# V of all four head pairs in one product of 512 columns: a change to a hybrid attention and state-space layer

## The chip, the core and the metric

The kernel runs on one core of a Trainium2 chip. The core has a matrix engine (TensorE, PE in the rows; its loads of stationary operands are PEld), a vector engine (VectorE, DVE), an activation engine (ScalarE, ACT), a general engine (GpSimd, POOL) and a queue engine (SyncE, SP) that only issues DMAs. Each engine runs its own list of instructions in order and waits on semaphores. The metric is device time in microseconds of one execution.

## The reference, cut to what matters

A decoder layer over 2048 tokens of width 1024. One projection gives Q, K and V for 3 attention groups of 8 heads of width 64 (windows 128, 512, 2048 with dilations 1, 4, 16), a gate `z_a`, the state-space input `u_s`, its gate `z_s`, and two merge gates:

```python
proj = einsum('bld,de->ble', h, w_in)
q, k, v = proj[..., :1536], proj[..., 1536:3072], proj[..., 3072:4608]   # (3 groups, 8 heads, 64) each
attn = _dilated_mixture(q, k, v) * silu(z_a)       # each group a causal dilated band, mixed by softmax sums
y = gelu(_s5(u_s, ...)); y = y * sigmoid(y @ w_glu + b_glu) * silu(z_s)
out = (sigmoid(g_a) * (attn @ w_attn_up) + sigmoid(g_s) * (y @ w_ssm_up)) @ w_o
h = layer_norm(2**0.25 * h + out) * ln_g + ln_b
```

The change touches how V, of shape (tokens, 3 x 512), is computed, and when `u_s` and the two branch gates are.

## The kernel before, in words

Arithmetic is float32 by splitting: an operand is cast to a short form `hi`, the rest `lo = raw - hi` is kept beside it, and each product is three matmuls, hi x hi, hi x lo and lo x hi. The tokens are worked in two halves `h` of 1024. Both forms of the half's x lie in SBUF (`X["h", kt]`, `X["l", kt]`, eight tiles of 128 model channels).

**Weights** come as blocks of 128 x 1024 numbers (512 KB) from one list, `plan` (L724 to 740), strictly in its order. The class `Weights` (L124 to 203) loads a block into a ring of two raw tiles (`fetch`, the DMA is issued on ACT's queue, L137), casts it to `hi` in two halves of 512 columns on ACT (`part`, L172), and subtracts to `lo` on POOL (L175; in the last phase on DVE). `hi` and `lo` have rings of two as well. A consumer calls `take` for a block, and while it runs `ahead` (first half of the next block's split) and `ahead2` (second half, then the DMA of the block after that).

**A projection block** (`gemm`, L205 to 248) makes 128 output channels for the 1024 tokens: two halves of 512 tokens, 8 model tiles, 3 matmuls of 512 columns each, 48 in all, into one of two PSUM banks `proj` per half. A piece of work of 6 such matmuls is one unit, 1.296 us in the kernel's own account. Q, K, `u`, `z_a`, `z_s` and gates are such blocks.

**V** (`v_gemm`, L431 to 458) is transposed: x is stationary, the weight moves, tokens are the output rows. One call makes V of two head pairs (256 columns) for the half's eight token tiles, from two weight blocks: block one holds model tiles 0 to 3, block two 4 to 7. Four token tiles share two banks, so that block one feeds 48 matmuls of 256 columns before block two is wanted. It is called for pairs 0 and 2 of each group, 12 times; results go through tile `th` to DRAM (`vD`), and each pair's job loads its 128 columns from there (`load_v`), into its tile `VV`.

**The jobs.** For each half, pair (0 to 3) and group (0 to 2), `job_proj` (L363) makes V if the pair is even, Q, then K (into tile `KC`); ACT casts and DVE subtracts out of PSUM (L398, L400). `job_attn` does the attention of a job in ten steps: scores (L595, L597), row maximum on DVE (L602), exp on ACT (L606), transposes on PE (L614), copies on ACT and DVE (L616, L617), PV (L625). The generator `interleave` (L261) deals out a job's projections (`bulk`) and the attention of the job before (`side`, 16.0 units) so that both end together: this fixes the order on every engine's list, and the side goes first where they tie. The main loop (L959 to 983) puts one `z` block into each job of the odd pairs. So a job of an even pair has V, Q and K, and one of an odd pair Q, K and a `z` block.

**The start.** `first_blocks` makes two `u` blocks while x is loaded and split; then come two more `u` blocks and the job (0, 0) without attention. Beside them DVE builds the tables of the state-space branch (`s5_tables`), a chain of some 200 small instructions, dealt out by `interleave` from the 17th unit on.

## Time and profile before

| | |
|---|---|
| time, median of 3 runs | 2165.84 us (2164.9 to 2165.98) |
| the profiled execution's own time | 2166.9 us |
| its span, first to last instruction | 2165.1 us |
| PE busy | 2136.9 us, 99% of the span |
| DVE, ACT, POOL busy | 1191.5, 1007.5, 701.4 us |
| mean granted TensorE clock | 0.998 |
| V products (L446), 2304 matmuls of 256 columns | busy 221.0 + 218.3 + 217.2 us |

The rows give start, duration, engine and line of an instruction, what it writes and reads, and in square brackets the idle time before it and what ended that. Matmuls overlap, so a matmul's duration (0.28 or 0.39 us) says little; what one costs is the distance from its start to the next one's. "ACTq" and "SPq" are DMA issues.

### The profile page before, as it was taken

The page shows a single profiled execution, that of the slowest core. Times are in us where ns is not written, and L with a number is a line of the kernel's source. Part 1 is how long each engine was busy: PE and PEld are TensorE (multiplying, and loading weights), DVE is VectorE, ACT ScalarE, POOL GpSimd, SP SyncE. Part 2 cuts the span into 40 slices and gives each one's busy share as a digit, 9 for nine tenths or more (in the row PEclk, how much of TensorE's full clock was granted, in tenths as well). Part 3 has the DMA queues.
Part 4 walks back from the last instruction along what each step waited for, and adds up shares of the span by engine and source line. Part 5 has one row for each costly group of instructions (what it writes and reads, how often), then busy time and mean ns, then how long its engine had stood idle before and what let it go on. Part 6 is the DMA issues. An engine that isn't in the chain of part 4 may idle for free. (4 is left out here: it accounts for less than half of the span.)

```text
span 2165.1 us, 32183 instructions
## 1 busy us (share of the span) xinstructions
PE 2136.9 (99%) x11440; PEld 1822.2 (84%) x11440; DVE 1191.5 (55%) x3064; ACT 1007.5 (47%) x2355; POOL 701.4 (32%) x587
## 2 busy tenths in 40 slices
PE   8999999999999999999999999999999999999998
PEld 6998889998888999888998888888888878888786
DVE  6644554445553244555445555258887784358725
ACT  3255665556554355665555665233433362232222
POOL 2322253253342234243243352411100004322643
PEclk9999999999999999999999999999999999999999
DMA  6323344344374333434344334554345463533721
GB/s 177 112 92 99 109 127 127 95 127 118 104 218 111 94 101 122 124 101 110 98 140 112 110 108 119 171 169 137 113 147 162 123 216 127 161 112 117 262 88 78
DMA packets 227569, 278.12 MB, mean 128 GB/s; under 512 B 89553, under 2 KB 175441, under 8 KB 227409
## 3 DMA queue, kind: packets, MB, share of 16 engines
q10 hardware_dynamic: 91776, 143.81, 21.7%
q1 hardware_dynamic: 135632, 132.25, 20.7%
q8 instruction: 91, 1.49, 0.3%
q14 instruction: 70, 0.57, 0.1%
HBM read 189.24 MB, written 74.19 MB: 122 GB/s over the span
## 5 line engine op out<-in xcount | busy, mean ns | idle before, releaser
L215 PE MATMUL proj<-xh,whi 128*128 128x512 f32 x1600 | 645.5, 403 | 1.2 <-ACT gt L719 1.2
L215 PE MATMUL proj<-xh,wlo 128*128 128x512 f32 x1600 | 628.5, 393 | 0.0
L215 PE MATMUL proj<-xl,whi 128*128 128x512 f32 x1600 | 626.0, 391 | 0.0
L175 POOL TENSOR_TENSOR wlo<-wraw,whi 128x512 fp32r<-128x512 f32 (+1 forms) x266 | 353.5, 1340 | 533.4 <-ACT whi L172 505.6
L215 PEld LDWEIGHTS proj<-xh,wlo 128*128 128x128 f32 x1600 | 300.2, 188 | 65.5
L215 PEld LDWEIGHTS proj<-xh,whi 128*128 128x128 f32 x1600 | 301.6, 189 | 54.4 <-issue 1.5
L215 PEld LDWEIGHTS proj<-xl,whi 128*128 128x128 f32 x1600 | 301.3, 188 | 51.3
L606 ACT ACTIVATE Sx<-Sx,st 128x256 f32<-128x256 f32 (+1 forms) x384 | 181.3, 473 | 263.7 <-DVE st L602 253.3
L633 POOL TENSOR_TENSOR og<-ot 128x128 f32<-128x128 f32 x192 | 88.2, 459 | 534.5 <-DVE ot L632 522.5
L172 ACT CAST whi<-wraw 128x512 fp32r<-128x512 f32 (+1 forms) x328 | 194.8, 617 | 117.4 <-PE ob L1406 43.3
L617 DVE TENSOR_TENSOR PT<-tr,PT 128x512 fp32r<-128x512 f32 (+1 forms) x192 | 118.9, 619 | 221.2 <-ACT PT L616 221.0
L446 PE MATMUL proj<-whi,xh 128*128 128x256 f32 x768 | 221.0, 288 | 0.0
L446 PE MATMUL proj<-wlo,xh 128*128 128x256 f32 x768 | 218.3, 284 | 0.9 <-POOL wlo L175 0.8
L446 PE MATMUL proj<-whi,xl 128*128 128x256 f32 x768 | 217.2, 283 | 0.0
L446 PEld LDWEIGHTS proj<-wlo,xh 128*128 128x128 f32 x768 | 146.8, 191 | 2.9 <-POOL wlo L175 2.4
L446 PEld LDWEIGHTS proj<-whi,xh 128*128 128x128 f32 x768 | 146.7, 191 | 0.1
L446 PEld LDWEIGHTS proj<-whi,xl 128*128 128x128 f32 x768 | 146.7, 191 | 0.0
L602 DVE CUSTOM_DVE_ANT_0 Sx<-sca,bias 128x256 f32<-128x256 f32 (+1 forms) x192 | 74.6, 388 | 105.3 <-PE sca L597 101.9
L632 DVE TENSOR_TENSOR ot<-ob,ot 64x256 f32<-64x256 f32 x192 | 81.0, 422 | 83.5 <-ACT ot L630 72.8
L632 DVE TENSOR_TENSOR ot<-oa,ot 64x256 f32<-64x256 f32 x192 | 81.0, 422 | 74.5 <-ACT ot L630 63.0
L614 PE MATMUL tr<-ident,Sx 128*128 128x128 f32 x664 | 109.9, 276 | 5.6 <-ACT Sx L606 5.1
L400 DVE TENSOR_TENSOR KC<-proj,KC 64x512 fp32r<-64x512 f32 x96 | 66.1, 688 | 82.9 <-ACT KC L398 82.0
(319 smaller groups left out, 3779.0 us busy)
## 6 DMA issues: line engine op xcount, KB each, us to landing
wraw<-in_w_in_dram ACTq DMA_DIRECT2D x102, 512.0 KB
ld<-gD SPq DMA_DIRECT2D x32, 512.0 KB
gD<-gt ACTq DMA_DIRECT2D x27, 512.0 KB
wraw<-in_w_v_dram ACTq DMA_DIRECT2D x24, 512.0 KB
vD<-th ACTq DMA_DIRECT2D x48, 256.0 KB
cB<-coefD SPq DMA_DIRECT2D x48, 256.0 KB
VV<-vD SPq DMA_DIRECT2D x16, 512.0 KB
xr<-in_xT_dram SPq DMA_DIRECT2D x16, 512.0 KB
```

Of the source, the lines that this page charges most:

```text
L172: A.copy(hi[:, c], raw[:, c])
L175: eng.tensor_tensor(lo[:, c], raw[:, c], hi[:, c].bitcast(F32), op=OP.subtract)
L215: T.matmul(ps, w[:, wc], m(kt)[:, cols], start=kt == 0 and n == 0, stop=3 * kt + n == last)
L400: V.tensor_tensor(gdst(lo, g, t), gsrc(ps[rows[s]], g), gdst(hi[rows[s]].bitcast(F32), g, t), op=OP.subtract)
L446: T.matmul(o, X[m, kt][:, 128 * i:128 * i + 128], w[half_k][wx][:, wc], start=kt == 0 and n == 0 and t % 2 == 0, stop=kt == 7 and n == 2, ...
L602: V.tensor_tensor_reduce(sx[:, s, lo:], ps2[s][:, lo:256], bias[:, s, lo:], scale=-0.125, scalar=3.0e38, op0=OP.add, op1=OP.min, accum_out ...
L606: A.activation(sx[:, s, lo:], sx[:, s, lo:], AF.Exp, scale=-1.0, bias=st[:, 0, s, c:c + 1], accum_out=st[:, 1, s, c:c + 1])
L614: T.transpose(p3[:, s, b], Sx[i][:, s, b * 128:(b + 1) * 128], ident)
L617: V.tensor_tensor(PT[:, 1, :, pos], p3[:, :, lo:], PT[:, 0, :, pos].bitcast(F32), op=OP.subtract)
L632: V.tensor_tensor(ot[half[s]], O[half[s], s], ot[half[s]], op=OP.add)
L633: P.tensor_tensor(og[pair, g][:, i * 128:(i + 1) * 128], ot[:, 0], ot[:, 1], op=OP.add)
```

## The change

V of all four pairs of a group becomes one product of 512 columns, once per half and group (6 calls), with four weight blocks of two model tiles each, in the same number of bytes. `v_gemm` begins with two token tiles, one bank each, and works block after block: 12 matmuls of 512 columns on block 0, then 12 on block 1, and so on; the blocks 1 to 3 are staged one at a time, each just ahead of the matmuls on the block before it. Block 1's `hi` and `lo` lie in the job's own `KC` tile, block 2's in its `VV` tile, blocks 0 and 3 in the rings. Then the six other token tiles are done with all four blocks in place. The second half of `lo` of the blocks 1 to 3 is made on DVE. The weights' order, `plan` and the main loop change: only two `u` blocks stand at the start of half 0 (one in half 1), the others and the `z` blocks stand one to a job of the pairs 1, 2 and 3, and none stands in job (2, 0) of half 0.

```diff
-        def begin(self):
+        def begin(self, home=None):
             raw, n = self.raws[len(self.splits)]
             left = len(self.plan) - len(self.splits)
-            if left <= 4:
+            if home is not None:
+                hi, lo = home[:, :HALF], home[:, HALF:2 * HALF]
+            elif left <= 4:
...
-                low(V if i < 2 and not k else P)
+                low(V if i < 2 and not k or k and i in self.shared else P)
...
-        if not odd:
-            yield from v_gemm(ev_v)
+        if not pair:
+            yield from v_gemm(vd, (j.KC.rearrange("k n s c -> k (n s c)"), j.V.rearrange("k i c -> k (i c)")))
...
+    def v_gemm(vd, homes):
+        n = vd.shape[1]
+        first = wts.i
+        wts.shared |= {first + 1, first + 2, first + 3}
+        w = [wts.take()]
+        homes = iter((*homes, None))
+        done = {}
+        def stage():
+            wts.begin(next(homes))
+            wts.finish()
+            w.append(wts.splits[-1])
+            wts.fetch(len(wts.splits) + 1)
+        def mms(ps, tt, kt):
+            wc = slice(n * (kt % 2), n * (kt % 2) + n)
+            for m, wx in (("h", 0), ("h", 1), ("l", 0)):
+                c = done[tt] = done.get(tt, 0) + 1
+                T.matmul(ps[:, :n], X[m, kt][:, 128 * tt:128 * tt + 128], w[kt // 2][wx][:, wc],
+                         start=c == 1, stop=c == 24)
...
+        ps = [ps_tile("proj", 2) for _ in range(2)]
+        for b in range(4):
+            if b < 3:
+                stage()
+            for kt, tt in ((0, 0), (0, 1), (1, 0), (1, 1)) if b < 3 else ((0, 0), (1, 0), (0, 1), (1, 1)):
+                mms(ps[tt], tt, 2 * b + kt)
+                if b == 3 and kt:
+                    evac(tt, ps[tt])
+                if tt or b == 3 and kt:
+                    yield cost
+        wts.i = first + 4
+        for tt in range(2, 8):
+            ps = ps_tile("proj", 2)
+            for b in (0, 3, 1, 2):
...
+    BESIDE = {(1, 0): "a0", (1, 1): "u2", (1, 2): "a1",
+              (2, 1): "u3", (2, 2): "a2", (3, 0): "s0", (3, 1): "s1", (3, 2): "a3"}
+    extra = [BESIDE, {**BESIDE, (2, 0): "u1"}]
+    front = [2, 1]
...
-        ub = [u_block(0, b) for b in range(2, 4)]
-        interleave(chain([first_blocks(first_x(ap), [u_evac(0, b) for b in range(2)])] + ub
+        interleave(chain([first_blocks(first_x(ap), [u_evac(0, b) for b in range(2)])]
                          + [job_proj(ap, wts, 0, 0, 0)]), 8 * BLK, s5_tables(ap), 32.0)
...
-                        n += 2 if pair % 2 else 4
+                        n += 2 if pair else 6
...
-                        interleave(chain(bulk), n * BLK, pend, 16.0, 12 * 0.216 if g == 0 and pair % 2 else 0.0)
+                        interleave(chain(bulk), n * BLK, pend, 16.0, 12 * 0.216 if (pair, g) == (1, 0) else 0.0)
```

The order on PE at the start of V in job (0, 1) of half 0, before. `whi_1049` and `wlo_1050` are weight block one, `whi_1140` block two, `xh0`, `xl0` model tile 0 of x; "..." stands for the same on other tiles of x.

```order
L597 MATMUL scb_1122<-KC_603,QLb0_600 128x128
L446 MATMUL proj_1144<-whi_1049,xh0_191 128x256
L446 MATMUL proj_1144<-wlo_1050,xh0_191 128x256
L446 MATMUL proj_1144<-whi_1049,xl0_192 128x256
...
L595 MATMUL sca_1186<-KC_603,QA_597 128x256
...
L614 MATMUL tr_1209<-ident_71,Sx_1127 128x128 x2
L446 MATMUL proj_1144<-whi_1140,xh4_275 128x256
L446 MATMUL proj_1144<-wlo_1141,xh4_275 128x256
```

The same place in the changed kernel; `whi_943` is block 0, `KC_1032` block 1, `VV_1033` block 2, `whi_1072` block 3, and `hi` and `lo` of a block in `KC` or `VV` have one name.

```order
L617 MATMUL scb_1016<-KC_376,QLb0_373 128x128
L446 MATMUL proj_1034<-whi_943,xh0_185 128x512
L446 MATMUL proj_1034<-wlo_944,xh0_185 128x512
L446 MATMUL proj_1034<-whi_943,xl0_186 128x512
...
L446 MATMUL proj_1034<-KC_1032,xh2_229 128x512 x2
...
L446 MATMUL proj_1034<-VV_1033,xh4_269 128x512 x2
...
L615 MATMUL sca_1086<-KC_376,QA_370 128x256
...
L446 MATMUL proj_1034<-whi_1072,xh6_308 128x512
```

Between the first matmul on one weight block and the first on the next there were 48 matmuls of 256 columns, a step's scores and two transposes; now there are 12 of 512 columns, and scores and transposes only in and after block 2.

ACT's list at the same place, before:

```order
L398 CAST KC_603<-proj_1042 64x4x128 x2
L391 CAST VV_604<-VV_604 128x8x2x64
L398 CAST KC_603<-proj_1079 64x4x128 x2
L606 ACTIVATE Sx_1127,st_1118<-Sx_1127,st_1118 128x128 x2
L172 CAST whi_1140<-wraw_1067 128x512 x2
L137 DMA wraw_1172<-in_w_in_dram 128x1024
```

and in the changed kernel:

```order
L399 CAST KC_376<-proj_973 64x4x128 x2
L626 ACTIVATE Sx_1021,st_1012<-Sx_1021,st_1012 128x128 x2
L174 CAST KC_1032<-wraw_961 128x512 x2
L137 DMA wraw_1040<-in_w_v_dram 128x1024
L174 CAST VV_1033<-wraw_1040 128x512 x2
L137 DMA wraw_1058<-in_w_v_dram 128x1024
L174 CAST whi_1072<-wraw_1058 128x512 x2
L137 DMA wraw_1078<-in_w_in_dram 128x1024
```

The first weight cast stands where it stood, behind the K casts and the exps of the attention's first step; two more loads and casts of weight blocks now follow it at once, each cast reading what the load just ahead of it brings.

DVE's list at the start of the program, before (the `L94` rows end the split of x, the `PT` rows begin the tables):

```order
L94 TENSOR_TENSOR xl6_315<-og_282,xh6_314 128x1024
L94 TENSOR_TENSOR xl7_331<-og_300,xh7_330 128x1024
L797 TENSOR_SCALAR PT_223<-PT_223 128x32
L795 TENSOR_SCALAR PT_223<-PT_223 128x32 x3
L822 SCALAR_TENSOR_TENSOR PT_223<-PT_223 128x32
```

and in the changed kernel:

```order
L94 TENSOR_TENSOR xl7_325<-og_294,xh7_324 128x1024
L177 TENSOR_TENSOR KC_376<-wraw_267,KC_376 128x512
L827 TENSOR_SCALAR PT_217<-PT_217 128x32
L825 TENSOR_SCALAR PT_217<-PT_217 128x32 x3
...
L844 COPY PT_217<-PT_217 128x32
L815 TENSOR_TENSOR PT_217<-PT_217 128x32
L177 TENSOR_TENSOR VV_377<-wraw_384,VV_377 128x512
L177 TENSOR_TENSOR wlo_450<-wraw_435,whi_449 128x512
```

The second half of block 1's `lo` now stands ahead of the whole table chain, and those of blocks 2 and 3 stand behind its first 28 rows of the list.

## Rows read from the trace of the kernel before

**Rows 1.** The page's head and its list of engines: busy time, share, instructions.

```profile
span 2165.1 us, 32183 instructions
PE 2136.9 (99%) x11440; PEld 1822.2 (84%) x11440; DVE 1191.5 (55%) x3064; ACT 1007.5 (47%) x2355; POOL 701.4 (32%) x587
```

**Rows 2.** Waits of PE, whole span: engine, line, waited for, us, times, longest.

```profile
PE tr L614 <- ACT Sx L606: 5.1, 4, 1.3
PE proj L446 <- POOL wlo L175: 0.8, 3, 0.3
```

**Rows 3.** Timeline of PE: first matmul of u2, of V, and of the following Q.

```profile
31.82 0.39 PE L215 MATMUL proj<-xh,whi 128*128 128x512 f32 x1
...
53.59 0.28 PE L446 MATMUL proj<-whi,xh 128*128 128x256 f32 x1
...
76.62 0.40 PE L215 MATMUL proj<-xh,whi 128*128 128x512 f32 x1
```

**Rows 4.** Timeline, all engines, start of V in job (0, 1), half 0.

```profile
98.63 1.18 ACT L398 CAST KC<-proj 64x512 fp32r<-64x512 f32 x2 [3.20 <-PE proj L215]
...
98.83 0.33 PE L446 MATMUL proj<-whi,xh 128*128 128x256 f32 x1
...
99.84 1.39 DVE L400 TENSOR_TENSOR KC<-proj,KC 64x512 fp32r<-64x512 f32 x2 [4.04 <-ACT KC L398]
...
102.12 0.40 ACT L606 ACTIVATE Sx<-Sx,st 128x128 f32<-128x128 f32 x1 [2.31 <-DVE st L602]
...
102.40 0.34 ACTq L137 DMA_DIRECT2D wraw<-in_w_in_dram  x1
...
102.91 1.13 ACT L172 CAST whi<-wraw 128x512 fp32r<-128x512 f32 x2
...
103.64 1.30 POOL L175 TENSOR_TENSOR wlo<-wraw,whi 128x512 fp32r<-128x512 f32 x1 [3.74 <-issue]
```

**Rows 5.** Timeline of ACT near the end, weight blocks cast as they land.

```profile
2089.30 0.34 ACTq L137 DMA_DIRECT2D wraw<-in_w_o_dram  x1
...
2092.89 0.62 ACT L172 CAST whi<-wraw 128x512 fp32r<-128x512 f32 x1 [2.51 <-DMA wraw<-in_w_o_dram]
2092.89 0.33 ACTq L137 DMA_DIRECT2D wraw<-in_w_o_dram  x1
...
2096.81 0.62 ACT L172 CAST whi<-wraw 128x512 fp32r<-128x512 f32 x1 [2.79 <-DMA wraw<-in_w_o_dram]
```

**Rows 6.** Timeline, all engines, first weight block after the first two u blocks.

```profile
37.66 0.62 ACT L172 CAST whi<-wraw 128x512 fp32r<-128x512 f32 x1 [0.59 <-ACT th L678]
37.76 0.92 ACTq L137 DMA_DIRECT2D wraw<-in_w_v_dram  x1
...
38.18 0.61 ACT L172 CAST whi<-wraw 128x512 fp32r<-128x512 f32 x1
...
38.41 1.29 POOL L175 TENSOR_TENSOR wlo<-wraw,whi 128x512 fp32r<-128x512 f32 x1 [6.04 <-DMA uD<-th]
```

**Rows 7.** Timeline of DVE: the tables' first row, row 28, one beside POOL, the last.

```profile
25.16 0.17 DVE L797 TENSOR_SCALAR PT<-PT 128x32 f32<-128x32 f32 x1
...
34.06 0.42 DVE L785 TENSOR_TENSOR PT<-PT 128x32 f32<-128x32 f32 x2
...
38.49 1.25 DVE L795 TENSOR_SCALAR PT<-PT 128x32 f32<-128x32 f32 x1
...
85.66 0.25 DVE L795 TENSOR_SCALAR PT<-PT 128x128 f32<-128x128 f32 x1
85.82 0.68 DVE L400 TENSOR_TENSOR QLa<-proj,QA 64x512 fp32r<-64x512 f32 x1
```

**Rows 8.** Timeline of ACT in half 1, start of V in jobs (0, 0) and (0, 2).

```profile
705.64 0.59 ACT L678 COPY th<-proj 128x512 f32<-128x512 f32 x1 [0.27 <-PE proj L215]
...
706.82 0.62 ACT L172 CAST whi<-wraw 128x512 fp32r<-128x512 f32 x1 [0.59 <-ACT th L678]
...
807.96 1.19 ACT L398 CAST KC<-proj 64x512 fp32r<-64x512 f32 x2 [2.40 <-PE proj L215]
...
813.09 1.12 ACT L172 CAST whi<-wraw 128x512 fp32r<-128x512 f32 x2
```

**Rows 9.** Windows over pairs 1 and 2 of half 0: length, PE busy (matmuls), clock, DMA.

```profile
208.79:339.99 131.20, 129.57 (x675) 1.00 0.44 122
339.99:502.55 162.56, 162.29 (x1100) 1.00 0.38 115
```

**Rows 10.** Instructions on the weight tiles: count, duration in ns least/median/most, first and last start.

```profile
L175 DVE TENSOR_TENSOR wlo<-wraw,whi x62: 426/685/3442, 3.5 to 1768.9; 128x512 fp32r<-128x512 f32 x60, 128x256 fp32r<-128x256 f32 x2
```

More of the change, by code (lines that the diff above doesn't have):

```diff
@@ L72, in layer_kernel @@
     tabD = dram.tile([128, 1472], F32, name="tabD")
-    vD = [[[dram.tile([HALF, 256], F32, name=f"vD{h}{p}{g}") for g in range(3)] for p in range(2)] for h in range(2)]
+    vD = [[dram.tile([HALF, 512], F32, name=f"vD{h}{b}") for b in range(3)] for h in range(2)]
     zaD = [[dram.tile([128, HALF], F32, name=f"zaD{h}{p}") for p in range(NPAIR)] for h in range(2)]
@@ L127, in __init__ @@
             self.open = False
-            self.late, self.todo = range(0), []
+            self.late, self.todo, self.shared = range(0), [], set()
         def fetch(self, upto):
@@ L373, in job_proj @@
         ka, kb = (j.KC[:, 2:, s] for s in range(2))
[L374 to L375 removed]
+        vd = vD[h][g]
         def load_v():
[L379 removed]
+            c = slice(128 * pair, 128 * pair + 128)
             dst = j.V[:, :, 64:192].bitcast(F32)
@@ L429, in job_proj @@
         jobs.append(j)
-    def v_gemm(evac):
-        w = [wts.take(), None]
-        wts.ahead()
-        for grp in range(2):
-            ps = [ps_tile("proj", 2).rearrange("t (i c) -> t i c", i=2) for _ in range(2)]
-            for half_k in range(2):
-                if grp == 0 and half_k == 1:
-                    w[1] = wts.take()
-                for t in range(4):
-                    o = ps[t // 2][:, t % 2]
-                    for k4 in range(4):
-                        kt = 4 * half_k + k4
-                        wc = slice(k4 * 256, (k4 + 1) * 256)
-                        for n, (m, wx) in enumerate((("h", 0), ("h", 1), ("l", 0))):
-                            i = 4 * grp + t
-                            T.matmul(o, X[m, kt][:, 128 * i:128 * i + 128], w[half_k][wx][:, wc],
-                                     start=kt == 0 and n == 0 and t % 2 == 0, stop=kt == 7 and n == 2,
-                                     skip_group_check=True)
-                    if (grp, half_k) in ((0, 0), (1, 1)):
-                        if t == 0:
-                            wts.ahead()
-                            if grp == 0:
-                                wts.finish()
-                        if t == 1:
-                            wts.ahead2()
-                    if half_k and t % 2:
-                        evac(2 * grp + t // 2, ps[t // 2])
-                    yield 6 * 0.216
@@ new lines, in v_gemm, with evac @@
+    def v_gemm(vd, homes):
[16 more added lines that the diff above has]
+                         start=c == 1, stop=c == 24)
+        def evac(tt, ps):
+            vs = wp.tile([128, 512], F32, name="th", tag="th", bufs=2)
+            A.copy(vs[:, :n], ps[:, :n])
+            A.dma_start(vd[128 * tt:128 * tt + 128], vs[:, :n])
+        cost = 6 * 0.216 * n / 512
+        ps = [ps_tile("proj", 2) for _ in range(2)]
[12 more added lines that the diff above has]
+            for b in (0, 3, 1, 2):
+                for kt in range(2):
+                    mms(ps, tt, 2 * b + kt)
+                if tt == 7 and b == 0:
+                    wts.ahead()
+                if tt == 7 and b == 1:
+                    wts.ahead2()
+                if b != 2:
+                    yield cost
+            evac(tt, ps)
+            yield cost
@@ L722, in gate_block, with extra_block @@
         return xgemm(wts, ev, outer)
+    BESIDE = {(1, 0): "a0", (1, 1): "u2", (1, 2): "a1",
+              (2, 1): "u3", (2, 2): "a2", (3, 0): "s0", (3, 1): "s1", (3, 2): "a3"}
+    extra = [BESIDE, {**BESIDE, (2, 0): "u1"}]
+    front = [2, 1]
+    def extra_block(h, nm):
+        b = int(nm[1])
+        return {"a": za_block, "s": zs_block, "u": u_block}[nm[0]](h, b)
     plan = []
     for h in range(2):
-        plan += [w_in[40 + b] for b in range(4)]
+        plan += [w_in[40 + b] for b in range(front[h])]
         for pair in range(NPAIR):
             for g in range(3):
-                if pair % 2 == 0:
-                    plan += [w_v[pair // 2, g, k] for k in range(2)]
+                if not pair:
+                    plan += [w_v[g, c] for c in range(4)]
                 plan += [w_in[12 * m + g * 4 + pair] for m in range(2)]
-                if pair % 2:
-                    plan.append((w_in[36 + pair - 1], w_in[44 + pair // 2], w_in[36 + pair])[g])
+                nm = extra[h].get((pair, g))
+                if nm:
+                    plan.append(w_in[{"a": 36, "s": 44, "u": 40}[nm[0]] + int(nm[1])])
         plan += [w_in[44 + b] for b in range(2, 4)]
@@ L965, in layer_kernel @@
         for h in range(2):
-            bulk = [u_block(1, b, b == 0) for b in range(4)] if h else []
+            bulk = [u_block(1, b, b == 0) for b in range(front[1])] if h else []
             n = len(bulk)
```

15 lines of the change are left out of this document (4 added, 11 removed).

## The prediction

> **What bounds the kernel now.** I read the engines' busy times first: PE is busy for 99% of the span, no other engine for more than 55% [rows 1]. The waits of PE say the same from the other side: in attention and projections it waits 5.1 us for exps, in four places, and 0.8 us for a weight's `lo`, in three [rows 2]. So a matmul saved is time saved, and a wait added to PE is time lost; what the other engines do costs something only where PE comes to wait for it. The profiled execution took 2166.9 us on its own clock, 1.06 us above the median of the runs; I sum against it and take 1.06 off at the end. A difference under 0.2% (4.3 us) can't be told from none here.
>
> **Part 1, the matmuls.** The timeline gives what a matmul costs as the distance between starts. From 31.82 to 53.59 us PE runs 96 matmuls of 512 columns (u2, u3) and nothing else: 21.77/96 = 0.2268 us. From 53.59 to 76.62 it runs 192 of 256 columns (V): 23.03/192 = 0.1199 us [rows 3]. Two narrow ones cost 0.2398, one wide one 0.2268, so 0.0130 us is won for each of the 1152 pairs: **-15.0 us**, all on PE, the engine that bounds. The Trainium skill, TensorE: Matmul & The Clock Gate, section Back-to-back issue gap, states 262 cycles for 256 columns and 518 for 512, which is 2.5 ns a pair at 2.4 GHz; that would make 2.9 us of this term and 2204 of my time. The trace does not agree (13.0 ns at a granted clock of 1.00), and the measurement decides.
>
> **Part 2, weights that come too late.** Before, block one fed 48 matmuls (5.8 us) and a step of attention before block two was wanted. Now block 0 feeds 12 wide ones, 12 x 0.2268 = 2.72 us, and the order puts nothing else between. When is block 1 there? ACT's list has the cast at the same place as before, so rows of before tell [rows 4]. V starts at 98.83. ACT casts K from 98.63, DVE subtracts it from 99.84, then makes the first scores' maximum, which ACT's exp awaits until 102.12; the first weight cast starts at 102.91, 4.08 after V's start. POOL begins `lo` at 103.64 and needs 1.30 for a half: 6.11 after V's start. The matmul hi x lo is the second on a block, so PE waits from 2.72 to 6.11 less one matmul: **3.2 us**. Block 1 is used up at 6.11 + 11 x 0.2268 = 8.6.
> Block 2's load can only be issued behind block 1's cast on ACT's list (at 3.57, since issues run ahead of the casts: 102.40 in the row). From issue to the cast of what it brings the end of the program shows 3.59 and 3.92 us [rows 5]; I take 3.75. So cast at 7.3, `lo` 2.03 later (4.08 to 6.11) at 9.4, a wait of 9.4 - 8.6 - 0.2 = 0.6. Then 2.5 for the block, 0.5 for four score matmuls, 0.2 for transposes: 12.6. Block 3: issue at 7.3, cast at 11.1, `lo` at 13.1, wait 0.3. Sum for this V product, **4.0 us**, and as much for job (0, 2), which has the same list.
> [...]
> In half 1 the cast comes later: in job (0, 2), 5.13 behind K's casts against 4.28 in rows 4 [rows 4, 8], so 0.85 more: **4.8**; job (0, 1) I put between at **4.3**. Job (0, 0) of half 1 has no K before it but a `u` block, whose copy and store put the cast 1.18 behind the copy's start [rows 8]; now two copies stand there, so 2.36 + 0.2 after V's start, `lo` at 4.6, first wait 1.4 (PE has a PV pair besides), later ones about 1.1: **2.5**.
>
> **Part 3, the start.** V now begins where u2 did, at 31.82. ACT is then held by the stores of the two `u` blocks: it casts the next weight block at 37.66, POOL has half its `lo` at 39.70 [rows 6]. PE has used up block 0 at 34.54: wait 4.9. On DVE, the second half of block 1's `lo` now stands ahead of the state-space tables, so these start not at 25.16 but after 38.79 + 0.69 = 39.5 [rows 6, 7, 10], and the second half of block 2's stands behind their first 28 rows, which took from 25.16 to 34.48 [rows 7]: done at 39.5 + 9.3 + 0.7 = 49.5. Block 2 finishes 1.1 after that, at 50.6, block 3 at 53.3, where four blocks without waits would end at 31.82 + 10.89 = 42.7: **10.6 us**. The tables' rest took 34.48 to 85.91 and now starts at 50.2: it ends at 101.6, and the two Q subtractions behind it (0.68 each) at 103.0. They free the PSUM bank that K's first half needs, which PE reaches at 31.82 + 240 x 0.2268 + 10.6 = 96.9: a further wait of 6.1 at face value. It can be less: a DVE instruction of 0.18 took 1.25 beside POOL's subtraction [rows 7], and POOL now has fewer. Bounds 0 and 6.1; I take **4**, nearer to the face value, since POOL still works on every weight block of that stretch, on three of them for a half.
>
> **Part 4, pair 2 without V, `u` and `z` dealt anew.** The number of blocks is the same, so no matmul is added. But attention is then spread over 3 blocks per job, not over V, Q and K, and pairs 1 and 2 show what that costs [rows 9]. Pair 1: 131.20 us less 432 x 0.2268 is 33.2 for attention and its waits. Pair 2: 162.56 less 576 x 0.1199 less 288 x 0.2268 is 28.2. It has 7 small matmuls fewer (0.8 us). So 4.2 us more in a half, **+8.5** for both; bounds 0 (the `u` blocks need no tanh) and 12 (job (2, 0) of half 0 has only Q and K beside attention). The 18 half subtractions taken from POOL and put on DVE, and the stores of `u` moved from the start into pairs 1 and 2, I cost at nothing: DVE is busy 55%, and the queue's loads there are wanted a whole block later. If that cover is gone, it is within the bound of 12. The old waits for `lo` go: **-0.8** [rows 2].
>
> **Sum.** New waits in V: 14.6 + 4.0 + 4.0 + 2.5 + 4.3 + 4.8 = 34.2. With the other terms -15.0 + 34.2 + 8.5 - 0.8 = +26.9; 2166.9 + 26.9 - 1.1 = 2192.7, so 2192 us.
>
> **Rivals.**
> (a) *Only the gain remains, and it gets faster.* If blocks 1 to 3 are split before PE wants them, since their homes in `KC` and `VV` are free early, V costs no wait: 2165.8 - 15.8 + 0 to 8.5 gives 2150 to 2158. It decides at block 1: its `lo` would have to be there 2.9 us after V's start, and not 6.1. For it: raw block and home are free by then. Against it: ACT's list puts the cast behind exps that end at 4.1. Chance 0.08.
> (b) *Only the first wait of each V product remains*, because the loads of blocks 2 and 3 come early and the tables give way: 4.9 + 3.2 + 3.2 + 1.4 + 3.5 + 4.0 = 20.2, less 15.8, plus 0 to 8.5: 2170 to 2178. For it: 0.6 and 0.3 us are small beside a scatter of 0.3 in the load. Against it: the tables' delay at the start hangs on an order that is fixed. Chance 0.14, a third of it within 0.2%.
> (c) *More starves.* The loads of blocks 2 and 3 meet the stores of the carried K and V and take 1 us longer each in five products, the tables cost the full 6.1, pair 2 the full 12: 10 + 2 + 3.5 more, up to 2208. For it: a load there would be issued while these stores run. Against it: it takes several at once. Chance 0.12.
> (d) *It doesn't do what it says* (products stay at 256 columns): excluded by the order, which shows 1152 matmuls of 512.
>
> **How the numbers follow.** My forecast, 2180 to 2204, has 0.66. The range of 8 in 10 leaves out (a), the lower part of (b) and the top of (c): 2173 to 2208. Slower by over 0.2%: forecast, (c) and two thirds of (b), with a little off for what I don't see: 0.86. Within 0.2%: 0.06. Faster: 0.08.
>
> **What will show it.** Part 1: V matmuls that start 0.227 apart in the six later token tiles. Part 2: in each V product gaps in PE before the second matmul on `KC`, of 3 to 4 us, ended by POOL, and smaller ones on `VV` and on block 3. Part 3: at about 34.5 us PE idle until 39.7, again until 49.5, ended by DVE, and the tables' last row near 100 us. Part 4: waits of transposes for exps in pair 2 like those in pair 1. The prediction is wrong if the first cast on `KC` comes within 1 us of V's start, or if the gaps are there and later waits shrink by as much.

## The result, and the profile after

| | before | after |
|---|---|---|
| time, median | 2165.91 us | 2190.23 us |
| ratio, 95% interval | 1 | 1.0115 (1.0103 to 1.0127) |
| span of the profiled execution | 2165.1 us | 2187.8 us |
| mean granted TensorE clock | 0.998 | 0.995 |

The wide V makes the kernel 24.3 us slower, where 26 were forecast (2192). The head of the page after, against [rows 1]:

```profile
span 2187.8 us, 29933 instructions
PE 2140.0 (98%) x10288; PEld 1763.3 (81%) x10288; DVE 1203.7 (55%) x3082; ACT 1008.8 (46%) x2355; POOL 680.2 (31%) x569
```

PE runs 1152 matmuls fewer and is no less busy (2140.0 us for 2136.9). Its waits, against [rows 2] (engine, line, waited for: us, times, longest; L446 is V's matmul now, L174 and L177 the cast and the `lo` of a weight block, L401 the subtraction behind a product of Q or K):

```profile
PE proj L446 <- DVE KC L401: 6.5, 4, 1.6
...
PE proj L446 <- POOL KC L177: 4.3, 5, 0.9
PE proj L446 <- ACT KC L174: 3.8, 3, 3.3
PE proj L446 <- DVE VV L177: 3.8, 1, 3.8
...
PE tr L634 <- ACT Sx L626: 2.5, 2, 1.3
PE proj L446 <- POOL VV L177: 2.4, 3, 0.8
PE sca L615 <- DVE st L622: 2.0, 1, 2.0
```

Every entry on L446 is new. The one on top is no wait for a weight. The timeline at the start of V in job (0, 1), to be laid beside [rows 4], shows both kinds (start, duration, engine, line, idle before it and what ended that):

```profile
109.90 1.17 ACT L399 CAST KC<-proj 64x512 fp32r<-64x512 f32 x2 [3.19 <-PE proj L217]
...
111.11 1.39 DVE L401 TENSOR_TENSOR KC<-proj,KC 64x512 fp32r<-64x512 f32 x2 [3.98 <-ACT KC L399]
...
113.67 0.33 ACTq L137 DMA_DIRECT2D wraw<-in_w_v_dram  x1
...
114.18 1.13 ACT L174 CAST KC<-wraw 128x512 fp32r<-128x512 f32 x2
114.92 1.27 POOL L177 TENSOR_TENSOR KC<-wraw,KC 128x512 fp32r<-128x512 f32 x1 [3.73 <-issue]
...
117.33 0.62 ACT L174 CAST VV<-wraw 128x512 fp32r<-128x512 f32 x1 [2.02 <-DMA wraw<-in_w_v_dram]
```

V starts at 110.10. The cast of block 1 comes 4.08 later and its first half of `lo` is done 6.09 later, both as the prediction had them from the old trace. But PE has stood before that: V's fourth matmul opens the second token tile's PSUM bank, in which the second half of K still lies until VectorE has subtracted it, at 112.50. That costs 1.8 us in four of the six products, counted from start to start (the list above, which goes by idle time, has 1.6). Block 1 is used up later by as much, so the wait for its `lo` is shorter by as much.

The windows at the start of the program show a third thing (length, busy us and count of PE, PEld, DVE, ACT, POOL, then the granted clock, DMA's share, GB/s):

```profile
37.50:38.80 1.30, 0.44 (x1) 0.12 (x1) 0.86 (x1) 0.41 (x1) 1.27 (x1) 1.00 0.98 148
38.80:42.00 3.20, 3.16 (x8) 2.48 (x9) 2.79 (x14) 0.54 (x2) 0.00 (x0) 0.54 0.64 185
...
44.80:49.60 4.80, 1.04 (x4) 0.58 (x3) 4.42 (x16) 1.14 (x2) 1.26 (x1) 0.97 0.01 2
49.60:52.40 2.80, 2.80 (x8) 2.18 (x7) 2.39 (x13) 0.00 (x0) 0.00 (x0) 0.50 0.62 187
```

Behind the wait that ended at 37.4 us (3.3 us), and behind the one that ended at 48.9 (3.8), the clock is granted at its lower level, 1.2 of 2.4 GHz, for some 3 us, and each matmul then takes 0.43 in place of 0.23 us: 8 matmuls, 1.6 us more, twice in this product. That is a surcharge on waits which the prediction did not have.

**What is "lost" in the tables below.** From a job's start to the next job's, less its matmuls at the distances of undisturbed stretches: 0.2319 us for a wide V matmul (below), 0.1199 for a narrow one, 0.2268 for Q, K, `u` and `z`, 0.1185 and 0.1095 for attention's of 256 and 128 columns. What is left is waits, low clock and, beside attention, a little more distance between matmuls: there Q's and K's start 0.228 to 0.231 us apart, before and after the change alike.

### The profile page after: what moved, and what is told of

Its sections match the earlier page's. It is cut to its first block, busy times and chain, and to the rows that moved or that the text cites. A ratio compares the mean times of both kernels' runs of the same rounds, so it can differ in the third digit from the quotient of the medians.

```text
span 2187.8 us, 29933 instructions
## 1 busy us (share of the span) xinstructions
PE 2140.0 (98%) x10288; PEld 1763.3 (81%) x10288; DVE 1203.7 (55%) x3082; ACT 1008.8 (46%) x2355; POOL 680.2 (31%) x569
## 4 chain that ended last, share of the span: by engine, by line
PE 55%; ACT 2%; DVE 2%; DMA 1%; issue 1%; ACTq 0%; POOL 0%; POOLq 0%; SPq 0%; DVEq 0%
PE proj L217 30%; PE proj L1377 8%; PE proj L1435 2%; PE tr L1435 2%; PE proj L446 2%; PE tr L634 2%; PE oa L645 1%; PE sca L1435 1%; PE scb L1435 1%; PE oa L1435 1%; PE ob L1435 1%; PE ob L645 1%; PE sca L1138 1%; PE scb L1205 1%; PE scb L1204 1%
## 5 line engine op out<-in xcount | busy, mean ns | idle before, releaser
L177 POOL TENSOR_TENSOR wlo<-wraw,whi 128x512 fp32r<-128x512 f32 (+1 forms) x236 | 315.4, 1347 | 547.3 <-ACT whi L174 515.2
L174 ACT CAST whi<-wraw 128x512 fp32r<-128x512 f32 (+1 forms) x304 | 179.9, 616 | 111.0 <-PE ob L1435 43.9
L636 ACT CAST PT<-tr 128x512 fp32r<-128x512 f32 (+1 forms) x192 | 99.5, 518 | 18.7 <-PE scb L617 5.0
L634 PEld LDWEIGHTS tr<-ident,Sx 128*128 128x128 f32 x664 | 79.2, 141 | 24.2 <-ACT Sx L626 12.2
L401 DVE TENSOR_TENSOR KC<-proj,KC 64x512 fp32r<-64x512 f32 x96 | 66.1, 689 | 53.3 <-ACT KC L399 52.6
L650 ACT COPY ot<-ob 64x256 f32<-64x256 f32 x192 | 70.4, 367 | 44.3 <-PE ob L645 38.4
L177 DVE TENSOR_TENSOR wlo<-wraw,whi 128x512 fp32r<-128x512 f32 (+1 forms) x68 | 51.9, 770 | 70.6 <-ACT whi L174 70.2
L650 ACT COPY ot<-oa 64x256 f32<-64x256 f32 x192 | 70.4, 367 | 34.7 <-PE oa L645 25.3
L1383 DVE SCALAR_TENSOR_TENSOR ld<-ld,proj 128x512 f32<-128x512 f32 x64 | 43.9, 686 | 75.7 <-PE proj L1377 75.3
```

Source lines behind the costliest of these rows:

```text
L174: A.copy(hi[:, c], raw[:, c])
L177: eng.tensor_tensor(lo[:, c], raw[:, c], hi[:, c].bitcast(F32), op=OP.subtract)
L634: T.transpose(p3[:, s, b], Sx[i][:, s, b * 128:(b + 1) * 128], ident)
L636: A.copy(PT[:, 0, :, pos], p3[:, :, lo:])
L650: A.copy(ot[half[s]], O[half[1 - s], s])
```

## Experiments

All times are medians; the kernel before took 2164.9 to 2165.9 us beside them.

### 1. Block 0's weights in place of the late ones

```diff
-  T.matmul(ps[:, :n], X[m, kt][...], w[kt // 2][wx][:, wc], ...)
+  T.matmul(ps[:, :n], X[m, kt][...], (w[kt // 2] if tt == 7 else w[0])[wx][:, wc], ...)
```

> In all six V products the token tiles 0 to 6 multiply by the weights of block 0 in place of blocks 1 to 3 (V is then wrong); blocks 1 to 3 are still loaded, cast and subtracted, by the same engines at the same places, so only PE's waits for them go. Theory, late weights: PE loses 40.5 us in the V products against the bare pitch; what stays is the wait for the PSUM bank of the second token tile, 1.8 us in four of the six products. In the product at the start (13.1 us lost) PE arrives earlier at K's bank, which is freed by Q's subtractions on VectorE behind the state-space tables; these end at 93.2 us as they do now, PE is there at 31.3 + 240 x 0.2268 = 85.7, so some 9 us of the 13 come back as a wait there. 2190.2 - 27.4 (five products: 27.4 lost, less 7.2 that stays = 20.2) gives 2190.2 - 20.2 - 4 = 2166, near the kernel before. Rival 1, the tables have given way and nothing comes back: 2157. Rival 2, the weights' lateness costs little and the time is lost to ACT's and POOL's extra work: 2188 to 2191.

The kernel leaves out the products with blocks 1 to 3 in seven of eight token tiles. Measured: 2186.77 us, ratio 1.0102 (1.0087 to 1.0117). The weights' lateness seems to cost 3.5 us, and the first theory is off by 20. PE's waits say where the time is:

```profile
PE proj L446 <- ACT th L451: 12.9, 6, 7.8
PE proj L446 <- DVE KC L401: 6.5, 4, 1.7
```

PE no longer waits for weights, but for `th`, the copies that empty the banks of token tiles 0 and 1. ACT's timeline at the start of the program shows why these are late:

```profile
41.88 0.62 ACT L174 CAST VV<-wraw 128x512 fp32r<-128x512 f32 x1 [3.47 <-DMA wraw<-in_w_v_dram]
...
45.54 1.14 ACT L174 CAST whi<-wraw 128x512 fp32r<-128x512 f32 x2 [2.52 <-DMA wraw<-in_w_v_dram]
49.54 0.33 ACTq L137 DMA_DIRECT2D wraw<-in_w_in_dram  x1
49.97 0.58 ACT L451 COPY th<-proj 128x512 f32<-128x512 f32 x1 [3.29 <-DVE VV L177]
```

The copy stands on ACT behind the casts of all three blocks, each of which waits for its load, and behind the issue of the next load, whose buffer VectorE's `lo` has to free. So PE goes on where the weights were late, and stands at the next thing that the same queue does. The experiment had taken away one of two waits on one chain. That rival 2's number came out does not make it right: it said that the lateness is cheap. The next experiment takes the chain itself away.

### 2. The chain taken out of the way

As in 1, and the loads, casts and subtractions of blocks 1 to 3 stand beside tiles 2, 3 and 4:

```diff
-            if b < 3:
-                stage()
...
             ps = ps_tile("proj", 2)
+            if tt < 5:
+                stage()
             for b in (0, 3, 1, 2):
```

> As in e1_block0 token tiles 0 to 6 use block 0's weights alone (V is wrong), but blocks 1 to 3 are now loaded and split beside tiles 2, 3 and 4, so that neither PE nor the copies of tiles 0 and 1 on ACT stand behind them. Theory, one chain on ACT (load issued behind a cast, cast behind its load, copies behind the casts) costs the V products their time, whoever waits for it: of the 34.6 us that the six V products lose against a wide V matmul's own pitch of 0.2319 us, only the waits for the second token tile's bank stay, 4 x 1.8 = 7.2, and up to 4 for K's bank behind the tables: 2190.2 - 34.6 + 7.2 = 2163, to 2167. Rival 1, the waits come from ACT's whole load of casts beside attention and only move to tiles 3 to 5: 2178 to 2186. Rival 2, the weights play no part: 2187.

Measured: 2169.49 us, ratio 1.0019 (1.0009 to 1.0029), a little over the 2163 to 2167 expected: 20.7 us gone, 17.3 of them against experiment 1, with the same number of loads, casts and subtractions. Lost in the V products of half 0 and half 1: 5.3, 1.9, 1.6 and 0.1, 1.9, 1.8, in place of 12.1, 3.9, 5.2 and 4.6, 4.1, 4.7: 12.6 for 34.6, where 7.2 to 11 were expected. The 5.3 at the start are the wait that the prediction had feared there, now that PE comes early: 3.4 us for Q's subtraction behind the tables.

```profile
PE proj L217 <- DVE QLb L401: 3.4, 1, 3.4
```

So the chain on ACT (load issued behind a cast, cast behind its load, copies behind the casts) is what V's waits come from.

### 3. The pitch of the wide matmul

```diff
-                T.matmul(ps[:, :n], ..., w[kt // 2][wx][:, wc], ...)
+                for q in range(2):
+                    T.matmul(ps[:, 256 * q:256 * q + 256], ..., w[kt // 2][wx][:, wc][:, 256 * q:256 * q + 256], ...)
```

> Same program, each V matmul of 512 columns written as two of 256 with the same weights and the same bank. Theory, pitch: two narrow ones take 0.2398 us and a wide one 0.2268, 1152 times, so the gain of 15.0 us of the wide matmuls is lost: 2205; a little less (2202) where a wait for weights ends at a fixed time and swallows it. Rival, the price of an issue gap as a page of the Trainium skill has it (TensorE: Matmul & The Clock Gate, Back-to-back issue gap): 2.5 ns a pair, 2193.

Measured: 2198.58 us, ratio 1.0153 (1.0138 to 1.0168): 8.4 us more than with wide matmuls, between the two expectations of 15.0 and 2.9. The starts of token tile 2 and of Q in job (0, 0) bound 144 wide matmuls in the changed kernel, and here 288 narrow ones. First the changed kernel, then this one:

```profile
54.50 0.39 PE L446 MATMUL proj<-whi,xh 128*128 128x512 f32 x1
...
87.90 0.40 PE L217 MATMUL proj<-xh,whi 128*128 128x512 f32 x1
```

```profile
56.27 0.28 PE L447 MATMUL proj<-whi,xh 128*128 128x256 f32 x1
...
90.80 0.39 PE L217 MATMUL proj<-xh,whi 128*128 128x512 f32 x1
```

33.40/144 = 0.2319 us for a wide one, 34.53/288 = 0.1199 for a narrow one. The narrow one costs what [rows 3] said. The wide one does not cost the 0.2268 of a `u` block: 1152 x (0.2398 - 0.2319) = 9.1 us are won, not 15.0.

Why 0.2319? In experiment 2 the moving columns of tiles 2 to 6 come from one pair of `whi`/`wlo` alone, and its 120 matmuls run from 43.18 to 70.38 us:

```profile
43.18 0.39 PE L446 MATMUL proj<-whi,xh 128*128 128x512 f32 x1
...
70.38 0.39 PE L446 MATMUL proj<-whi,xh 128*128 128x512 f32 x1
```

27.20/120 = 0.2267, the price of a `u` block. The next kernel takes block 1's weights, which lie in `KC`, for all of tiles 2 to 6:

```diff
-  w[kt // 2][wx][:, wc]
+  w[1 if 1 < tt < 7 else kt // 2][wx][:, wc]
```

> The changed kernel, with block 1's weights in place of all four in token tiles 2 to 6 (V is then wrong there); loads, casts and waits stay. It asks what the pitch of a wide V matmul rests on. In the changed kernel these tiles read their 512 moving columns in turn from whi/wlo, KC and VV, and the matmuls of the first product start 0.2319 us apart; in e5_late, where they come from one pair of whi/wlo alone, 0.2273. Here they come from KC alone. Theory, the place: matmuls that move KC stay at 0.233 to 0.236. Rival, the turning from tile to tile: 0.227. The time itself: 2190, at most 3 up or down.

Measured: 2193.09 us in a single run. Its 120 matmuls:

```profile
56.41 0.40 PE L446 MATMUL proj<-KC,xh 128*128 128x512 f32 x1
...
84.42 0.39 PE L446 MATMUL proj<-whi,xh 128*128 128x512 f32 x1
```

28.01/120 = 0.2334. It is the place, then, and not the turning from tile to tile: in the first product, columns moved out of `KC` cost 0.007 us a matmul more than those out of one `whi` and `wlo`. In the five products beside attention the difference is smaller. Between two V matmuls of tiles 2 to 6 that follow each other, the starts there lie 0.228 to 0.230 us apart out of the one pair (experiment 2), 0.232 to 0.233 in the changed kernel and 0.233 to 0.234 out of `KC`: the place costs 0.003 to 0.005 there, since beside attention the columns out of the one pair cost 0.002 to 0.003 more than without it, and those out of `KC` at most 0.001. What about the place does it (address, size of the tile, what else is written near it) no run here tells. Experiments 1 and 2 both had the cheaper columns, some 2 us in the six products, so the 17.3 us between those two are the chain's alone.

### 4. The start: which engine, and where `u` stands

GpSimd takes both halves of `lo` in the first product:

```diff
-        wts.shared |= {first + 1, first + 2, first + 3}
+        if first > 2:
+            wts.shared |= {first + 1, first + 2, first + 3}
```

> In the first V product alone all six half subtractions of blocks 1 to 3 stand on GpSimd, none on VectorE. Theory, the lo halves stand behind the tables on VectorE: the wait of 3.9 us at 44.8 us ends, GpSimd has that half by about 44.4; block 1's second half comes 0.9 us later than now (1.4 us on VectorE against 1.3 more on GpSimd after its first half), and one stretch of low granted clock with it (about 1.5 us) goes: 2190.2 - 3.9 - 1.5 + 1 = 2186, 2184 to 2188. The tables begin at about 25 us again. Rival, the wait only moves to block 3, whose subtraction then stands behind four others on GpSimd: 2189 to 2191.

Measured: 2187.92 us, ratio 1.0101 (1.0084 to 1.0118); the first product loses 8.5 in place of 12.1, and the wait for VectorE is gone from the list. The time agrees with the theory, but lies only 2.3 us under the changed kernel, and the two intervals overlap; the job's own 3.6 us show it better.

In the other kernel all four `u` blocks of half 0 stand at the start again:

```diff
-    extra = [BESIDE, {**BESIDE, (2, 0): "u1"}]
-    front = [2, 1]
+    extra = [{k: v for k, v in BESIDE.items() if v[0] != 'u'}, {**BESIDE, (2, 0): "u1"}]
+    front = [4, 1]
```

> In half 0 the four u blocks stand at the start again, none in pairs 1 and 2; half 1 and the wide V stay. Theory: V of job (0, 0) then starts at about 53 us, ACT, GpSimd and the tables are out of its way, and of its 13.1 us some 2.5 stay, as in job (0, 0) of half 1: -10.6. Jobs (1, 1) and (2, 1) then spread attention over Q and K alone, as job (2, 0) does, which loses 4.65 us where (2, 1) loses 1.7: +3 each. Sum -4.6: 2185.6, 2182 to 2188. Rival 1, the dealing of u is harmless and the wide product starves alike wherever it stands: 2190 to 2196. Rival 2, the thin jobs cost nothing: 2179.

Measured: 2194.87 us, ratio 1.0135 (1.012 to 1.015): slower by 4.6, where the theory had it faster by as much. V's first product loses 6.2 in place of 12.1, 5.9 won, not 10.6: block 1 is there in time, blocks 2 and 3 are not, and the low clock comes behind their waits too. And a job with only Q and K beside attention costs more than I had put: (1, 1) loses 5.5 in place of 1.5 and (2, 1) 6.4 in place of 1.7, with 1.2 more in (1, 2): 9.9. The number is that of rival 1, the reason is not. Dealing `u` out into pairs 1 and 2 is worth more than it costs.

### 5. A cast moved ahead, nothing else

```diff
-  interleave(chain(bulk), n * BLK, pend, 16.0, 12 * 0.216 if (pair, g) == (1, 0) else 0.0)
+  interleave(chain(bulk), n * BLK, pend, 16.0,
+             12 * 0.216 if (pair, g) == (1, 0) else 0.0 if pair else 0.01)
```

> The changed kernel with one number changed: beside a V product the bulk's first step is ordered ahead of attention's first, so that ACT casts block 1 right behind K's copies, some 1.3 us after V's start in place of 4.1. Theory, the chain: block 1's lo at 3.3 after V's start, by when the second tile's bank (free at +2.5) already holds PE back; block 2's load is issued at 1.9, cast 5.6, lo 7.6, block 3 cast 9.9, lo 11.9 against a need near 11: the waits per product fall from 4.5 to about 2.8, in four products: 2190.2 - 7 = 2183, 2180 to 2186. Rival 1, the place of the first cast is all: only the bank's 1.8 stay, 2178. Rival 2, the loads are all: 2190.

Measured: 2188.31 us, ratio 1.0109 (1.0093 to 1.0124): hardly a gain, 1.9 for 7, with overlapping intervals. Jobs (0, 1) and (0, 2) lose 2.7 and 4.0 in half 0 and 2.6 and 6.1 in half 1, against 3.9, 5.2, 4.1 and 4.7. The chain did move, loads included. In job (0, 1) of half 0 (V's start, block 2's load, block 1's cast, and then the only wait on L446 in that job):

```profile
111.11 0.39 PE L446 MATMUL proj<-whi,xh 128*128 128x512 f32 x1
...
111.37 0.34 ACTq L137 DMA_DIRECT2D wraw<-in_w_v_dram  x1
...
112.50 1.14 ACT L174 CAST KC<-wraw 128x512 fp32r<-128x512 f32 x2
```

```profile
PE proj L446 <- DVE KC L401: 2.1, 1, 2.1
```

The load is issued 0.26 us after V's start in place of 3.57, the cast comes at 1.39 in place of 4.08, and PE waits for no weight there any more, nor in (0, 1) of half 1 and (0, 2) of half 0. But the wait for the bank, the same instruction on VectorE, grows from 1.6 to 2.1 us, and behind it the clock falls in both jobs (0, 2), where it had not, though not in the jobs (0, 1):

```profile
195.50:198.50 3.00, 3.00 (x9) 2.33 (x8) 1.24 (x3) 1.85 (x6) 1.28 (x1) 0.57 1.00 284
```

### 6. Blocks split ahead of V: does the wide V pay then?

```diff
+    def prestage(ap, h, g):
+        j = ready[h, g] = Job()
+        j.KC = ap.tile([128, 10, 2, 128], F32R, name="KC", bufs=2)
+        wts.begin(j.KC.rearrange("k n s c -> k (n s c)"))
+        wts.finish()
+        wts.fetch(len(wts.splits) + 1)
...
+                    if pre and (t, kt) == (1, 3):
+                        pre()
...
-            for kt, tt in ((0, 0), (0, 1), (1, 0), (1, 1)) if b < 3 else ((0, 0), (1, 0), (0, 1), (1, 1)):
+            for tt, k2 in ((0, 0), (0, 1), (1, 0), (1, 1)) if b == 0 else ((0, b), (1, b)) if b > 1 else ():
```

> Nothing left out. Block 1 of a V product is split beside the second half of the K product before it, into the K tile that is free by then (at the start blocks 0 to 2 beside the u blocks), and the first token tile multiplies by blocks 0 and 1 before the second opens its bank. Theory, the chain on ACT sets V's waits: blocks 0 and 1 feed 24 matmuls, 5.6 us; block 2's lo comes 6.1 us after V's start, as block 1's does now, block 3's some 3.9 later, at 10 against a need at 8.9. Waits of 0.3 and 1.0 in five products, 1 at the start, none for the bank: 7.5 in place of 34.6: 2163, 2159 to 2168. Rival 1, the earlier casts hold exps of attention back in the K product, 1 to 2 us in five places, and the tables are late at the start (4): 2169 to 2177. Rival 2, weights play no part: 2190.

Measured: 2166.48 us, ratio 1.0007 (0.9998 to 1.0017): 23.8 of the 24.3 us are back, and nothing is left out. The V products lose 1.1, 1.6, 1.8, 0.3, 1.1, 3.8, together 9.7 (7.5 expected). What PE still waits for in them:

```profile
PE proj L475 <- POOL VV L177: 2.1, 3, 0.9
PE proj L475 <- POOL wlo L177: 1.0, 3, 0.6
PE proj L475 <- ACT VV L174: 1.0, 1, 1.0
```

Four changes of order went on top: the bulk's first step ahead of attention's beside V, attention in job (1, 0) held back for two steps and then level, a little ahead in the thin job (2, 0), the hook of half 1's `u` block (the call that splits V's block 1 ahead) behind its copies. Held back means that attention starts when the projections have done the `lead`; level, that its share of the work done then follows theirs from zero and not from the `lead`.

```diff
-  b >= lead and s / side_total <= (b - lead) / (bulk_total - lead)
+  b >= lead and s / side_total <= b / bulk_total
...
-  pend, 16.0, 12 * 0.216 if (pair, g) == (1, 0) else 0.0)
+  pend, 17.2 if n == 2 else 16.0,
+  12 * 0.216 if (pair, g) == (1, 0) else 0.0 if pair else 0.01)
```

> e6_pre with four changes of order, nothing left out: the cast of block 2 goes ahead of the first scores on ACT (the bulk's first step before attention's), the hook of half 1's u block behind the copies of u, attention in job (1, 0) held back for two steps and then level with the others, in the thin job (2, 0) a little ahead, so that a maximum is not queued behind Q's subtractions on VectorE. Theory, each is a wait that the trace of e6_pre shows: 0.3 to 2.8 us each in four V products (block 2's lo by about 3.8 us after V's start, not 6.1, against a need at 5.6; its load for block 3 that much earlier), together -4.5; u block -0.9; two transposes in (1, 0) of 1.4 and 1.5, -2.9; one maximum of 2.1 with 1.5 of low granted clock behind it, -3.5. Sum -11.8: 2154.7, 2151 to 2159, faster than the kernel before by 0.3 to 0.65%. Rival, waits only move to the next exp or maximum, since attention's ops stay as many: 2162 to 2168.

Measured: 2163.74 us, ratio 0.9994 (0.9985 to 1.0003), 2.7 won for 11.8. Two of the four did what the trace had promised: V's jobs (0, 1) and (0, 2) now lose 0.4, 0.1 in half 0 and 0.4, 1.6 in half 1, and job (1, 0) 1.4 in each half in place of 2.8. Two turned round. The late hook put the whole chain of loads back: V's job (0, 0) of half 1 loses 4.5 in place of 0.3. And in (2, 0) the wait only changed its name, 5.9 lost for 4.7. So the next kernel has the hook where it was, and holds attention in (2, 0) back instead, by 1.3 steps and not level:

```diff
-  pend, 17.2 if n == 2 else 16.0, ...)
+  pend, 16.0, {(1, 0): 12 * 0.216}.get((pair, g), 7.8 * 0.216 if n == 2 else 0.0 if pair else 0.01), n > 2)
```

> e7_order with two of its four changes taken back or turned: the hook of half 1's u block stands ahead of the copies of u again, as in e6_pre, and attention in the thin job (2, 0) is held back by 1.3 steps of the bulk, not let ahead. Theory: in e7_order V's job (0, 0) of half 1 waits 0.8, 1.1 and 0.4 for block 1 and 0.4 and 1.2 for block 3, since the late hook delayed the whole chain of loads; in e6_pre it waits for nothing but 1.0 at the copy of u: -2.9. In (2, 0) scores, transposes and products of a step no longer meet Q's subtractions on VectorE: the waits of 0.5, 1.3 and 0.8 go, and what e6_pre has there, 2.1 and 1.5 of low clock, does not come back: -3 to -4. 2163.7 - 6.5 = 2157, 2154 to 2160. Rival, the thin job has too little work on PE and waits elsewhere: 2160 to 2162.

Measured: 2160.24 us, ratio 0.9974 (0.9965 to 0.9983): faster than the kernel before, at the edge of the 2154 to 2160 expected. V loses 4.2 us in all six products. But (2, 0) has 6.7 now, as the rival said, on these waits:

```profile
PE sca L645 <- DVE st L652: 3.7, 7, 1.4
...
PE oa L675 <- DVE PT L667: 1.2, 1, 1.2
```

Whose gain is it? The same holding back, put into the kernel before and with no wide V:

```diff
-  b >= lead and s / side_total <= (b - lead) / (bulk_total - lead)
+  b >= lead and s / side_total <= b / bulk_total
```

> The kernel before with one condition changed, nothing of the wide V: attention beside jobs (1, 0) and (3, 0) is held back for two steps and then level with the others, as e7_order does it in (1, 0). Theory: the two transposes in each of these four jobs that wait for exps (5.1 us in all in the trace of before), and 1 to 2 us of small waits with them, go; jobs (1, 0) of e7_order show 1.4 lost where e6_pre showed 2.8: 2165 - 5.5 = 2159.5, 2158 to 2162. Then as much of a gain of e9_best is not the wide V's. Rival, the exps are then waited for one step later: 2164 to 2166.

Measured: 2159.02 us, ratio 0.9971 (0.9959 to 0.9982). Its trace has no wait of transposes for exps any more ([rows 2] had 5.1 us); jobs (1, 0) and (3, 0) lose 0.8 and 0.8 in half 0, 1.4 and 1.4 in half 1, against 2.8, 2.7, 3.7, 3.0. One condition in the old kernel gives as much as the wide V with all its helpers, which have that condition too; the two cannot be told apart, so no gain of the wide V itself is shown.

The last kernel gave the thin job a third block, a gate block of the late stage:

```diff
-    extra = [BESIDE, {**BESIDE, (2, 0): "u1"}]
+    extra = [{**BESIDE, (2, 0): "g0"}, {**BESIDE, (2, 0): "u1"}]
...
-    plan += gate + gate + (glu + up + fin_o) * 2
+    plan += gate + gate[1:] + (glu + up + fin_o) * 2
```

> e9_best with a third block in the one thin job: gate block 0 of half 0, computed late in the program so far, is computed beside Q and K of job (2, 0), stored, and read back where the other gates are; attention there is not held back any more. Nothing is left out. Theory: job (2, 0) loses 6.7 us in e9_best beyond its matmuls, 4.7 in e6_pre, and jobs with three blocks beside the same attention lose 0.6 to 0.8: -5.9. The late stage has the same matmuls but for this block, and PE bounds it: 2160.2 - 5.9 = 2154.3, 2152 to 2157, under the kernel before with its hold-back changed (2159.0). Rival, the state-space work beside which the gate block stood takes as long as before and PE idles there instead: 2160.

Measured: 2162.95 us, ratio 0.9987 (0.9978 to 0.9996), 2.7 more than `e9_best` where 5.9 less were expected. Job (2, 0) loses 0.6, as expected, and the program has won 6.0 there. The rest, from job (3, 2) of half 1 on, should be shorter by the block, 10.9 us; it is by 3.8, and PE's waits there show a new entry:

```profile
PE oa L1114 <- DVE F L1105: 4.1, 2, 2.4
```

The block had been cover for the state-space work, so the rival holds, and the time lies above even its 2160.

## Why the prediction was right, point by point

| term | predicted | found |
|---|---|---|
| wide matmuls | -15.0 | -9.1 |
| V, job (0, 0), half 0, with K's bank | +14.6 | +12.1 |
| V, jobs (0, 1), (0, 2), half 0 | +4.0, +4.0 | +3.9, +5.2 |
| V, jobs (0, 0), (0, 1), (0, 2), half 1 | +2.5, +4.3, +4.8 | +4.6, +4.1, +4.7 |
| pair 2 | +8.5 | +8.0 |
| waits that go | -0.8 | -10.2 |
| sum | +26.9 | +23.3 |

The spans differ by 22.7, the medians by 24.3. (The prediction's own sum was 2192.7, put down as 2192.) In the last row but one, 2.6 were lost in pair 0's V jobs before, 7.3 went in pairs 1 and 3, 0.3 in `u` and `z`.

**Part 1 was mis-sized.** The step "one wide one 0.2268" took a wide matmul's price from a stretch with the weights stationary, x moving and no attention beside it. Turning the operands round costs nothing by itself (0.2267 in experiment 2). Columns out of `KC` cost more (0.2334), beside attention even those out of one pair do (0.228 to 0.230), and the mixture of the changed kernel is 0.2319: 9.1 us, not 15.0. The Trainium skill, TensorE: Matmul & The Clock Gate, section Back-to-back issue gap, whose figures are for matmuls by themselves, would have made it 2.9; the runs agree with neither.

**Part 2 held in sum, not in its parts.** 19.6 for the five products, 22.5 found. Cast and `lo` of block 1 came 4.08 and 6.09 us after V's start, as worked out, but the gap before the second matmul on `KC`, forecast at 3 to 4 us, was 0.9. The wait for the second tile's bank was not seen: the old order opened that bank after 24 narrow matmuls, 2.9 us, the new one after three wide ones, 0.7. It lies under the wait for block 1, so it adds little; the low clock, behind the waits in (0, 0) of half 1, was not seen either. Experiment 1 showed what the prediction also left out: with the weights there, the copies behind them on ACT would hold PE as long. From a load's issue to its cast it was 3.66 us (113.67 to 117.33) against the 3.75 taken.

**Part 3: right for the first waits, wrong for K's bank.** PE stood from 34.1 us, until ACT's cast at 37.4 and POOL's `lo` at 38.8 (39.7 forecast), and from 45.2, until VectorE's `lo`, as forecast; VectorE's half of `lo` for block 2, worked out to be done at 49.5, is so at 48.9:

```profile
37.94 1.39 DVE L177 TENSOR_TENSOR KC<-wraw,KC 128x512 fp32r<-128x512 f32 x1 [13.08 <-DMA uD<-th]
39.26 0.17 DVE L827 TENSOR_SCALAR PT<-PT 128x32 f32<-128x32 f32 x1
...
48.18 0.68 DVE L177 TENSOR_TENSOR VV<-wraw,VV 128x512 fp32r<-128x512 f32 x1
...
93.20 0.25 DVE L825 TENSOR_SCALAR PT<-PT 128x128 f32<-128x128 f32 x1
94.78 0.68 DVE L401 TENSOR_TENSOR QLa<-proj,QA 64x512 fp32r<-64x512 f32 x1 [1.33 <-ACT QB L399]
```

But the tables end at 93.4 and not at 101.6: their rest took 44 us and not the 51.4 of [rows 7]. The reason is in the trace. While GpSimd subtracts half a block, VectorE gets one small instruction done, in 1.2 to 1.3 us in place of 0.2:

```profile
84.61 2.60 POOL L177 TENSOR_TENSOR wlo<-wraw,whi 128x512 fp32r<-128x512 f32 x2 [37.49 <-ACT whi L174]
84.75 1.28 DVE L815 TENSOR_TENSOR arena<-PT 128x16 f32<-128x16 f32 x1
86.06 1.21 DVE L818 TENSOR_TENSOR PT<-PT,arena 128x16 f32<-128x16 f32 x1
87.17 0.18 DVE L815 TENSOR_TENSOR PT<-PT 128x16 f32<-128x16 f32 x1
```

Beside the rest of the tables stood ten such halves before, each with its one long VectorE instruction; now there are four. Six fewer, at 1.06 us each, are 6.4 of the 7.4 us. The prediction knew that POOL had fewer there, and took only 2.1 us off for it (from 6.1 to 4). Q's subtraction then waits for Q, not for the tables, and the 4 us at K's bank do not come; the low clock behind two waits gave 3 us in their place. Experiment 2 shows the wait as soon as PE is early enough.

**Part 4 held in its number, not in its sign.** The waits of transposes for exps that pair 2 was to show are not there; both that are left stand in pair 1. What it shows is the thin job that the prediction had named in its bound: (2, 0) of half 0 alone went from 0.2 lost in the old V job to 4.7, of which 2.0 are the wait of scores for a maximum on VectorE (the last entry of the list after) and about 1.5 the low clock behind it. The windows over pairs 1 and 2 of half 0, against [rows 9]:

```profile
271.18:401.92 130.74, 129.37 (x675) 107.72 (x673) 73.03 (x213) 81.49 (x222) 54.83 (x50) 1.00 0.46 124
401.92:523.78 121.86, 119.61 (x623) 99.57 (x623) 70.34 (x210) 78.70 (x217) 52.35 (x48) 0.99 0.44 120
```

**The old waits were under-sized.** "-0.8" counted only the waits for `lo`. Job (3, 0) is no longer held back for two steps, since the job before it now ends with a `z` block, and its exps come in time: 2.7 to 0.6 and 3.0 to 1.1 lost. The 5.1 us for exps stood in [rows 2], and I did not ask which of them the new dealing would touch. This error and that of part 1 are 9.4 and 5.9 us, with opposite signs. That the sum comes out better than its terms is luck.

**Rivals.** (a), 2150 to 2158, and (b) did not come; (a) decided at block 1's `lo`, and it was as late as said. Experiment 6 shows that (a) could be built, and that its times were too low: the pitch won 5.9 us less than (a) took, and V still lost 9.7 us there. Of (c) nothing came either: block 2's load took 3.66 us, the start lost 12.1 and pair 2 8.0.

## What to carry to other kernels

A wider product uses up its weights faster, and where one in-order queue issues the loads, casts them and empties the banks, all three come late together: an experiment that removes one wait only shows the next, so move the chain, not the wait. Price a matmul from one with its moving operand out of the same place and with the same work beside it. And before building helpers round a new product, ask of the old kernel which of its waits the helpers would also remove: here one condition there gave the same.
